# A hybrid attention, mLSTM and GLA layer: later decay broadcasts in the first block, a second buffer for convolution inputs, bias shifts spread over the gate projections

## The chip, the cores and the metric

The kernel runs on one core of a Trainium2 chip. The metric is device time in microseconds (us) of one execution, as the median of several runs. A core has TensorE (PE; its weight loads are shown apart as PEld), VectorE (DVE), ScalarE (ACT), GpSimd (POOL) and SyncE (SP), which here only issues DMAs. L123 is a line of the kernel before.

## What is computed

One layer on a sequence of 2048 rows of width 1024. All three head groups read the same normalised input, and their gated outputs go together through one output projection. Cut to its core:

```python
hn = rmsnorm(x, norm_g)
z = einsum('bsd,de->bse', hn, w_in)
(aq, ak, av, ag, mq, mk, mv, mo, mi, mf, mg, gq, gk, gv, ga, gg) = split(z)

# A: softmax attention over the own chunk of 64 and the 8 before, with a relative-position bias
y_a = band_chunk_attention(aq, ak, av, rel_bias) * silu(ag)

# B: mLSTM with exponential input gate, sigmoid forget gate and running-max stabiliser
qk = silu(causal_conv(concat([mq, mk]), conv_w))          # 4 taps along the sequence
y_b = sigmoid(mo) * head_rmsnorm(mlstm_chunkwise(mq_c, mk_c, mv, mi + b_i, mf + b_f), ml_norm_g) * silu(mg)

# C: gated linear attention with a decay for each key channel
log_alpha = log_sigmoid(ga @ w_alpha + b_alpha) / 16
y_c = head_rmsnorm(gla_chunkwise(gq, gk, gv, log_alpha), gla_norm_g) * silu(gg)

x = x + concat([y_a, y_b, y_c]) @ w_out
return rmsnorm(x, final_g)
```

## The kernel before

**Stages.** The first stage goes through the sequence in four blocks `q` of 512 rows. For each it makes the projections and runs the mLSTM and GLA recurrences in chunks of 128 rows; attention's queries, keys and values go to DRAM. The second stage does attention and the output projection block by block.

**Matmuls.** A projection is computed from high and low parts: the raw weights (128x1024 f32) are loaded by SyncE (L225), ScalarE casts them to the high part (L227), VectorE or GpSimd subtracts to get the low part (L228). Three matmuls for each of eight slices of the inner dimension then accumulate in a PSUM bank named `ip` (L236 to L238 in `proj_g`, L256 to L258 in `proj_t`). There are two `ip` banks, three buffers for raw weights and five for split ones. A bank is free again when its result has been read: by a copy (L513 and L515 for values, L547 for convolution inputs), a tanh (L486 in `sig_tile`) or a tanh and VectorE's product (L492 in `silu_tile`).

**Order.** PE's order is that in which the program is written. `Flow` weaves the recurrences, which are Python generators, into the projections: `flow.piece` counts PE's time and steps each chain that is due. On every other engine, SyncE among them, a list scheduler orders the instructions by priority and by its own estimate of when each is ready; what stands in `tc.high_priority` (casts, evacuations, raw loads) comes ahead, `tc.keep_in_program_order` pins an instruction, and `tc.issue_after(ins)` puts what is traced inside behind `ins` on `ins`'s engine. The hardware then runs each engine's list in that order.

**A block** runs, in program order: `proj_z` (GLA's query and key), `proj_v` (values for mLSTM, L256 to L258), `proj_gg` (GLA's gate), the second half of `proj_v`, `proj_m` (the mLSTM's queries and keys with their convolution), `prep_x` (loads of the next block's `x`, squares on ScalarE at L280, a diagonal `dg` at L285), then `proj_gm` (output gates `mo` and `mg`, three each), `prep` (the next block's input) and `proj_a` (attention's projections). `gates` of a block runs at its beginning; it writes the decay rows to `nm_d` in DRAM (L458) and turns gate rows by four transposes (L476). In the last block the order differs a little.

**What the change touches:**

- `load_dd` (L645 to L648), inside `mlstm`: broadcasts one chunk's six decay rows from `nm_d` to all 128 partitions (`dd`, 384 KB). L663 works on each of the six, L665 takes the exponential, L682 multiplies the scores. `mlstm` loads chunk 0 and 1 when it is first stepped, which is in `proj_gm` behind the load of `mo0`'s weights; in the scheduler's hands these DMAs may go out as soon as `nm_d` is written.
- `proj_m` (L540 to L561): for each of six tiles a copy of the bank to `zb`, 3 + 512 columns (L547), its three leading columns by GpSimd (L549 or L551), the last three kept for the next block (L552), the first tap on ScalarE (L554), three taps on VectorE (L556), tanh (L558) and product (L559). `zb` is the tile `u` with one buffer.
- `g_tile` (L203): tiles of 512 columns from `gpool`, which has five buffers, for `gates`, `prep`, `prep_x` and `prep_first`.
- `bias_rel` (L609 to L616), called in block `q == 1` ahead of `proj_gm`: loads attention's bias tile `bt` and shifts its six heads on ScalarE (L615), then GpSimd fills the masked corner (L616). Attention reads `bt` in the second stage.
- `gsel` (L434, L441): selects the gate rows; 64 columns for the mLSTM's.
- `Kt` (L194): seven key tiles for GLA, of which the first four use 64 of 128 columns (L831, L839).

Of the kernel before, what the change touches and what calls it, by code (L numbers as in the profile page):

```python
# [8 lines left out]
FP32 = mybir.dt.float32  # L9
FR = mybir.dt.float32r  # L10
AF = mybir.ActivationFunctionType
# [5 lines left out]
P = 128  # L17
D = 1024
KT = D // P
QT = 512  # L20
ST = 256
L = 128
# [79 lines left out]
def trunk_kernel(ctx: ExitStack, tc: tile.TileContext, xT, x, w_f, w_t, w_o, w_gates, norm_g, conv_w,  # L102
                 gate_sel, one_row, bias, ml_g, gla_g, final_g, out):
    nc = tc.nc
# [8 lines left out]
    nm_d = dram.tile([NQ, MH, QT], FP32, name="nm_d")  # L113
# [29 lines left out]
    with ExitStack() as pa_:  # L143
# [20 lines left out]
        onerow = one.tile([P, 1], FP32, name="onerow")  # L164
        gsel = one.tile([P, P + 64], FP32, name="gsel")
        zero6 = one.tile([P, 1], FP32, name="zero6")[G0:G0 + MH]
# [26 lines left out]
        glg = one.tile([P, 2], FP32, name="glg")  # L193
        Kt = one.tile([P, 7, P], FP32, name="Kt")  # L194
        nc.gpsimd.memset(Kt, 0.0)
        Qb = one.tile([P, 8, 4, 16], FP32, name="Qb")
# [6 lines left out]
        def g_tile(shape):  # L203
            return gpool.tile(shape, FP32, name="g")

# [13 lines left out]
        def load_w(src, k):  # L219
            if early_w:  # L220
                return early_w.pop(0)
            w = w_tile(k)
            with tc.high_priority(offset=AHEAD):
                raw = wraws.tile([P, D], FP32, name="wraw")
                nc.sync.dma_start(raw, src)  # L225
                rv = raw.rearrange("p (k n) -> p k n", k=k)
                nc.scalar.copy(w[:, :, 0, :], rv)  # L227
                other().tensor_tensor(w[:, :, 1, :], rv, f32(w[:, :, 0, :]), op=ALU.subtract)  # L228
            return w
# [13 lines left out]
        def proj_f(name, X):  # L243
            out_ = []
            for _ in proj_g(name, X, out_, 4):
                flow.piece(12 * 0.227)
            return out_[0]
# [183 lines left out]
        def gates(q, g1, R):  # L431
            t0 = q * QT
            pb = bank("pw")
            nc.tensor.matmul(pb[0:64], gsel[:, P:P + 64], g1, start=True, stop=True)  # L434
            gi = g_tile([P, QT])[G0:G0 + MH]
# [47 lines left out]
        def sig_tile(ps):  # L483
            th = ev.tile([P, QT], FP32, name="e")
            with tc.high_priority(offset=AHEAD):
                nc.scalar.activation(th, ps, AF.Tanh, scale=0.5)  # L486
            return th
# [52 lines left out]
        def proj_m(X):  # L540
            qk = big.tile([P, 6, QT], FP32, name="qk", bufs=1)
            tail = big.tile([P, 6, 3], FP32, name="tail")
            for b in range(6):
                ps = proj_f(("mq" if b < 3 else "mk") + str(b % 3), X)
                zb = big.tile([P, 3 + QT], FP32, name="u", bufs=1)
                with tc.high_priority(offset=AHEAD):
# [15 lines left out]

        def proj_gm(X):
            gm = big.tile([P, 3, QT], FP32, name="gm", bufs=1)
            for a in range(3):
                th = sig_tile(proj_f(f"mo{a}", X))
                nc.gpsimd.tensor_scalar(th, th, 1.0, mlg[:, a:a + 1], op0=ALU.add, op1=ALU.mult)
                sl = silu_tile(proj_f(f"mg{a}", X))
                nc.gpsimd.tensor_tensor(gm[:, a, :], th, sl, op=ALU.mult)
            return gm  # L570

# [37 lines left out]
        def bias_rel():  # L609
            bc = big.tile([P, AH], FP32, name="sm")  # L610
            nc.sync.dma_start(bc, bias[:, :, 256])
            nc.scalar.activation(bc, bc, AF.Copy, scale=-1.0)
            nc.sync.dma_start(bt, bias[:, :, 0:256])
            for h in range(AH):
                nc.scalar.activation(bt[:, h, :], bt[:, h, :], AF.Identity, bias=bc[:, h:h + 1])  # L615
            nc.gpsimd.memset(bt[0:64, :, 192:256], NEG)  # L616

        def m_tile(shape):
# [22 lines left out]
        def mlstm(q, qk, vs, R, held=None):  # L641
# [3 lines left out]
            def load_dd(c):  # L645
                dd = d_tile()
                nc.sync.dma_start(dd, nm_d[q, :, c * L:(c + 1) * L].partition_broadcast(P))
                return dd  # L648
# [162 lines left out]
        def gla(q, vg, gg, G, held=None):  # L811
            for sub in range(2):
# [7 lines left out]
                for c in range(2):  # L820
# [9 lines left out]
                    for i in range(1, 8):  # L830
                        nc.gpsimd.tensor_tensor(Kt[:, i - 1, 0:16 * i].rearrange("p (b j) -> p b j", j=16), ko[:, c, 0:i, :],  # L831
                                                Dt[:, c, i, 1:1 + i].unsqueeze(2).broadcast_to([P, i, 16]), op=ALU.mult)
# [4 lines left out]
                    for i in range(1, 8):  # L837
                        w = 64 if i < 5 else P
                        nc.tensor.matmul(of_ps[0:w, 64 * i:64 * i + 64], Kt[:, i - 1, 0:w], Qb[:, i, :, :].rearrange("p h i -> p (h i)"),  # L839
                                         start=True, stop=True)  # L840
# [63 lines left out]
        for q in range(NQ):  # L904
# [34 lines left out]
            flow.need("gates")  # L939
            if q == 1:  # L940
                bias_rel()
            M = dict(R)
            flow.start("mlstm", mlstm(q, qk, vs, M))
            M["gm"] = proj_gm(X)
            R = {}
# [325 lines left out]
def _layout(inputs):  # L1271
# [34 lines left out]
    o["conv_w"] = np.ascontiguousarray(a["conv_w"][0].reshape(4, 6, P).transpose(2, 1, 0))  # L1306
    gs = np.zeros((4, 32, P + 64), np.float32)
    gs[:, 0:16, 0:P] = a["w_alpha"][0]
# [5 lines left out]
    gs[0, 28, P + 32:P + 32 + MH] = a["b_gates"][0][:MH][[0, 2, 4, 1, 3, 5]]  # L1314
    gs = gs.reshape(P, P + 64)
    o["one_row"] = np.zeros((P, 1), np.float32)
# [29 lines left out]
```

## Time and profile before

| what | value |
|---|---|
| median of the three runs | 1284.47 us |
| these runs | 1284.54, 1284.47, 1280.35 us |
| the profiled execution's own time | 1278.8 us |
| its span | 1276.9 us |
| PE's granted clock in it | 0.99 |

The span is the part of the execution in which the program's instructions run. Busy time of PE counts the modelled ends of pipelined matmuls. In a timeline row stand start, length, engine, line, operation, tiles written and read, shape and count, and in brackets how long the engine had been idle and which instruction ended the wait. Rows of one engine in a row with the same work are merged, and their length then spans them all. In the chain of waits, one follows back from the last instruction what released each step.

### The profile page before, as it was taken

How to read it: one execution, taken by the hardware profiler on the slowest of the kernel's cores; microseconds unless marked ns; L12 is line 12 of the kernel's file. 1: busy time of each engine (PE TensorE's matmuls, PEld its weight loads, DVE VectorE, ACT ScalarE, POOL GpSimd, SP SyncE). 2: the span in 40 equal slices, each digit the busy share in tenths (PEclk: the TensorE clock that was granted, in tenths of full speed). 3: DMA queues.
4: the chain of work that ended last, by engine and by line, in shares of the span. 5: the costliest groups of instructions: out<-in, count | busy, mean ns of one | idle time of the engine just before them, and what ended most of it. 6: DMA issues, size and time to landing. Idle time of an engine off the chain costs nothing.

```text
span 1276.9 us, 19361 instructions
## 1 busy us (share of the span) xinstructions
PE 1243.8 (97%) x6804; PEld 1008.3 (79%) x6804; DVE 813.7 (64%) x1869; ACT 590.1 (46%) x1097; POOL 592.2 (46%) x761
## 2 busy tenths in 40 slices
PE   9999999999999999999999999999989999999997
PEld 7777777778777788877778877887867888878886
DVE  6647736772675878266577766675577677666641
ACT  5635432562533346254333643332576565655631
POOL 3336663233666232276622446642364454454442
PEclk7999999999999999999999999999999999999999
DMA  7157344324733442472344233526886456555122
GB/s 246 27 158 259 111 124 150 118 73 131 258 96 114 143 129 66 136 260 88 108 138 124 84 127 98 138 72 175 282 258 205 156 181 207 165 184 172 50 83 82
DMA packets 100185, 184.31 MB, mean 144 GB/s; under 512 B 10592, under 2 KB 46304, under 8 KB 100088
## 3 DMA queue, kind: packets, MB, share of 16 engines
q1 hardware_dynamic: 95624, 174.95, 43.6%
q10 hardware_dynamic: 4464, 8.13, 1.7%
q8 instruction: 53, 0.87, 0.3%
q14 instruction: 44, 0.36, 0.1%
HBM read 147.35 MB, written 35.70 MB: 143 GB/s over the span
## 4 chain that ended last, share of the span: by engine, by line
PE 77%; DVE 8%; POOL 4%; DMA 4%; issue 3%; ACT 3%; SPq 0%; POOLq 0%; DVEq 0%; ACTq 0%
PE ip L236 11%; PE ip L238 10%; PE ip L237 10%; PE ip L256 4%; PE ip L1196 4%; PE ip L1198 4%; PE ip L1197 4%; PE ip L258 4%; PE ip L257 4%; PE s L1055 4%; PE tp L1115 3%; DVE qk L556 2%; PE w L1134 2%; PE ga L839 2%; PE w L1131 2%
## 5 line engine op out<-in xcount | busy, mean ns | idle before, releaser
L236 PE MATMUL ip<-x,w 128*128 128x512 f32 x784 | 318.8, 407 | 3.0 <-ACT u L547 2.7
L238 PE MATMUL ip<-x,w 128*128 128x512 f32 x784 | 306.4, 391 | 0.0
L237 PE MATMUL ip<-x,w 128*128 128x512 f32 x784 | 306.0, 390 | 0.0
L236 PEld LDWEIGHTS ip<-x,w 128*128 128x128 f32 x784 | 147.3, 188 | 46.8 <-issue 12.5
L238 PEld LDWEIGHTS ip<-x,w 128*128 128x128 f32 x784 | 147.2, 188 | 32.4
L237 PEld LDWEIGHTS ip<-x,w 128*128 128x128 f32 x784 | 147.5, 188 | 28.1 <-issue 1.4
L227 ACT CAST w<-wraw 128x1024 fp32r<-128x1024 f32 x126 | 131.7, 1046 | 31.4 <-PE ip L258 10.3
L228 POOL TENSOR_TENSOR w<-wraw,w 128x1024 fp32r<-128x1024 f32 x42 | 100.8, 2401 | 97.0 <-ACT w L227 97.0
L228 DVE TENSOR_TENSOR w<-wraw,w 128x1024 fp32r<-128x1024 f32 x84 | 114.6, 1366 | 45.5 <-ACT w L227 45.4
L1076 POOL TENSOR_SCALAR pt<-pt,sm 128x640 f32<-128x640 f32 (+2 forms) x96 | 72.2, 754 | 118.9 <-DVE sm L1075 92.5
L256 PE MATMUL ip<-w,x 128*128 128x512 f32 x256 | 102.2, 399 | 4.4 <-DVE e L492 2.9
L258 PE MATMUL ip<-w,x 128*128 128x512 f32 x256 | 99.8, 390 | 0.0
L257 PE MATMUL ip<-w,x 128*128 128x512 f32 x256 | 99.7, 390 | 0.0
L781 POOL TENSOR_TENSOR prd<-gk,zg 128x16 f32<-128x16 f32 (+7 forms) x112 | 67.1, 599 | 68.0 <-PE pw L787 62.0
L1074 ACT ACTIVATE pt<-pt,sm 128x640 f32<-128x640 f32 (+2 forms) x96 | 73.3, 763 | 48.3 <-DVE sm L1071 43.9
L1122 DVE TENSOR_TENSOR pl<-tp,ph 128x512 fp32r<-128x512 f32 (+1 forms) x108 | 71.9, 672 | 35.0 <-ACT ph L1121 34.8
L1055 PE MATMUL s<-kk,qq 128*128 128x256 f32 (+2 forms) x360 | 82.4, 314 | 2.3 <-DVE sm L1071 2.2
L778 POOL TENSOR_TENSOR gk<-gk,al 128x16 f32<-128x16 f32 (+14 forms) x120 | 69.6, 580 | 22.1 <-ACT al L755 14.6
L1121 ACT CAST ph<-tp 128x512 fp32r<-128x512 f32 (+1 forms) x108 | 60.3, 572 | 39.7 <-PE tp L1115 37.3
L486 ACT ACTIVATE e<-ip 128x512 f32<-128x512 f32 x44 | 26.2, 595 | 107.5 <-PE ip L238 91.5
L1055 PEld LDWEIGHTS s<-kk,qq 128*128 128x128 f32 x360 | 62.8, 190 | 16.1 <-DVE sm L1071 5.8
L556 DVE SCALAR_TENSOR_TENSOR qk<-u,cw,qk 128x512 f32<-128x512 f32 x72 | 65.7, 913 | 13.7 <-ACT qk L554 12.2
(342 smaller groups left out, 2483.4 us busy)
## 6 DMA issues: line engine op xcount, KB each, us to landing
wraw<-in_w_f SPq DMA_DIRECT2D x100, 512.0 KB, 3.6
wraw<-in_w_t SPq DMA_DIRECT2D x28, 512.0 KB, 3.6
qq<-q_d SPq DMA_DIRECT2D x48, 256.0 KB, 4.8
kk<-k_d SPq DMA_DIRECT2D x18, 512.0 KB, 6.5
vv<-v_d SPq DMA_DIRECT2D x18, 512.0 KB, 5.8
xraw<-in_xT SPq DMA_DIRECT2D x16, 512.0 KB, 8.5
xr<-in_x SPq DMA_DIRECT2D x16, 512.0 KB, 3.7
out<-xr ACTq DMA_DIRECT2D x31, 256.0 KB, 2.2
```

The source lines that it names most:

```text
L227: nc.scalar.copy(w[:, :, 0, :], rv)
L228: other().tensor_tensor(w[:, :, 1, :], rv, f32(w[:, :, 0, :]), op=ALU.subtract)
L236: nc.tensor.matmul(ps, w[:, k, 0, :], X[k][:, 0, :], start=(k == 0), stop=False)
L237: nc.tensor.matmul(ps, w[:, k, 0, :], X[k][:, 1, :], start=False, stop=False)
L238: nc.tensor.matmul(ps, w[:, k, 1, :], X[k][:, 0, :], start=False, stop=(k == KT - 1))
L256: nc.tensor.matmul(ps, X[k][:, 0, t], w[:, 0, :], start=(k == 0), stop=False)
L257: nc.tensor.matmul(ps, X[k][:, 0, t], w[:, 1, :], start=False, stop=False)
L258: nc.tensor.matmul(ps, X[k][:, 1, t], w[:, 0, :], start=False, stop=(k == KT - 1))
L556: nc.vector.scalar_tensor_tensor(acc, zb[:, i:i + QT], cw[:, b, i:i + 1], acc, op0=ALU.mult, op1=ALU.add)
L1055: nc.tensor.matmul(sp[:, :cn], qq[:, l, tt * P:(tt + 1) * P], kk[:, ko + c0:ko + c0 + cn], start=(l == 0), stop=(l == 1))
L1074: nc.scalar.activation(pt[:, :n], pt[:, :n], AF.Exp, bias=init, scale=-1.0, accum_out=sm[:, 2:3])
L1076: nc.gpsimd.tensor_scalar(pt[:, :n], pt[:, :n], sm[:, 3:4], 0.5, op0=ALU.mult, op1=ALU.mult)
```

## The change

Three edits alter an order or a buffer. In the first block the broadcasts of chunks 0 and 1 are issued behind the last raw weights that were asked for; of the six convolution inputs the odd ones come from `gpool` instead of `u`; and `bias_rel` becomes a generator that is stepped once ahead of the mLSTM and then twice for each of the three pairs of gate projections, so that each shift stands behind a tanh. The other edits make tiles smaller or wider: `g` tiles have 515 columns, `gsel` loses 16, and `Kt` becomes four tiles of 64 columns and three of 128.

```diff
-        gsel = one.tile([P, P + 64], FP32, name="gsel")
+        gsel = one.tile([P, P + 48], FP32, name="gsel")
...
-        Kt = one.tile([P, 7, P], FP32, name="Kt")
-        nc.gpsimd.memset(Kt, 0.0)
+        Kh = one.tile([P, 4, 64], FP32, name="Kh")
+        nc.gpsimd.memset(Kh, 0.0)
+        Kl = one.tile([P, 3, P], FP32, name="Kt")
+        nc.gpsimd.memset(Kl, 0.0)
+        Kt = [Kh[:, i] for i in range(4)] + [Kl[:, i] for i in range(3)]
...
         def g_tile(shape):
-            return gpool.tile(shape, FP32, name="g")
+            t = gpool.tile([P, 3 + QT], FP32, name="g")[:, 0:QT]
+            return t.rearrange("p (c t) -> p c t", c=shape[1]) if len(shape) > 2 else t
...
                 raw = wraws.tile([P, D], FP32, name="wraw")
-                nc.sync.dma_start(raw, src)
+                st["raw"] = nc.sync.dma_start(raw, src).ins
...
-            nc.tensor.matmul(pb[0:64], gsel[:, P:P + 64], g1, start=True, stop=True)
+            nc.tensor.matmul(pb[0:48], gsel[:, P:P + 48], g1, start=True, stop=True)
...
-                nc.scalar.activation(th, ps, AF.Tanh, scale=0.5)
+                st["th"] = nc.scalar.activation(th, ps, AF.Tanh, scale=0.5).ins
...
-                zb = big.tile([P, 3 + QT], FP32, name="u", bufs=1)
+                zb = gpool.tile([P, 3 + QT], FP32, name="g") if b % 2 else big.tile([P, 3 + QT], FP32, name="u", bufs=1)
...
-        def proj_gm(X):
+        def proj_gm(X, shift=None):
             gm = big.tile([P, 3, QT], FP32, name="gm", bufs=1)
             for a in range(3):
                 th = sig_tile(proj_f(f"mo{a}", X))
+                if shift:
+                    next(shift)
                 nc.gpsimd.tensor_scalar(th, th, 1.0, mlg[:, a:a + 1], op0=ALU.add, op1=ALU.mult)
                 sl = silu_tile(proj_f(f"mg{a}", X))
                 nc.gpsimd.tensor_tensor(gm[:, a, :], th, sl, op=ALU.mult)
+                if shift:
+                    next(shift)
             return gm
...
             for h in range(AH):
-                nc.scalar.activation(bt[:, h, :], bt[:, h, :], AF.Identity, bias=bc[:, h:h + 1])
+                yield
+                with tc.issue_after(st["th"]):
+                    nc.scalar.activation(bt[:, h, :], bt[:, h, :], AF.Identity, bias=bc[:, h:h + 1])
             nc.gpsimd.memset(bt[0:64, :, 192:256], NEG)
+            yield
...
                 dd = d_tile()
-                nc.sync.dma_start(dd, nm_d[q, :, c * L:(c + 1) * L].partition_broadcast(P))
+                with tc.issue_after(st["raw"]) if q == 0 and c < 2 else nullcontext():
+                    nc.sync.dma_start(dd, nm_d[q, :, c * L:(c + 1) * L].partition_broadcast(P))
...
-                        nc.tensor.matmul(of_ps[0:w, 64 * i:64 * i + 64], Kt[:, i - 1, 0:w], Qb[:, i, :, :].rearrange("p h i -> p (h i)"),
+                        nc.tensor.matmul(of_ps[0:w, 64 * i:64 * i + 64], Kt[i - 1], Qb[:, i, :, :].rearrange("p h i -> p (h i)"),
...
-            if q == 1:
-                bias_rel()
+            shift = bias_rel() if q == 1 else None
+            if shift:
+                next(shift)
             M = dict(R)
             flow.start("mlstm", mlstm(q, qk, vs, M))
-            M["gm"] = proj_gm(X)
+            M["gm"] = proj_gm(X, shift)
```

More of the change, by code (lines that the diff above doesn't have):

```diff
@@ L830, in gla @@
                     for i in range(1, 8):
-                        nc.gpsimd.tensor_tensor(Kt[:, i - 1, 0:16 * i].rearrange("p (b j) -> p b j", j=16), ko[:, c, 0:i, :],
+                        nc.gpsimd.tensor_tensor(Kt[i - 1][:, 0:16 * i].rearrange("p (b j) -> p b j", j=16), ko[:, c, 0:i, :],
                                                 Dt[:, c, i, 1:1 + i].unsqueeze(2).broadcast_to([P, i, 16]), op=ALU.mult)
@@ L1306, in _layout @@
     o["conv_w"] = np.ascontiguousarray(a["conv_w"][0].reshape(4, 6, P).transpose(2, 1, 0))
-    gs = np.zeros((4, 32, P + 64), np.float32)
+    gs = np.zeros((4, 32, P + 48), np.float32)
     gs[:, 0:16, 0:P] = a["w_alpha"][0]
@@ L1314, in _layout @@
     gs[0, 28, P + 32:P + 32 + MH] = a["b_gates"][0][:MH][[0, 2, 4, 1, 3, 5]]
-    gs = gs.reshape(P, P + 64)
+    gs = gs.reshape(P, P + 48)
     o["one_row"] = np.zeros((P, 1), np.float32)
```

## The prediction

> **What bounds the kernel now.** I read the page first, then the list of what TensorE waited for, then the timelines of the engines around each of its waits.
>
> ```profile
> span 1276.9 us, 19361 instructions
> PE 1243.8 (97%) x6804; PEld 1008.3 (79%) x6804; DVE 813.7 (64%) x1869; ACT 590.1 (46%) x1097; POOL 592.2 (46%) x761
> ```
>
> TensorE (PE) is busy for 97% of the span, its instruction order is written by hand, and the change removes none of its matmuls. So the time can only fall by the length of waits on PE, at most the 33.1 us between 1276.9 and 1243.8. Which waits these are is told by the waits of PE alone (who waited for whom, us in total, times, longest):
>
> ```profile
> PE ip L256 <- DVE e L492: 2.9, 1, 2.9
> PE ip L236 <- ACT u L547: 2.7, 2, 2.5
> ...
> PE ip L256 <- ACT vg L515: 1.4, 1, 1.4
> ```
>
> Beside them the list has mostly waits of the attention stage, which no line of the diff touches. These three rows are waits for one of the two `ip` banks in which projections accumulate: the engine that should empty the bank came late. Together they hold 7.0 us in four waits, and each has a cause that the diff names.
>
> Wait 1, in the first block. SyncE's timeline, ScalarE's, the chain of waits (start, length, what) and PE's timeline:
>
> ```profile
> 59.89 0.97 SPq L647 DMA_DIRECT2D dd<-nm_d  x2
> 61.60 0.35 SPq L225 DMA_DIRECT2D wraw<-in_w_t  x1
> ```
> ```profile
> 60.44 1.14 DVE w L228
> ...
> 61.60 8.03 DMA wraw<-in_w_t
> ```
> ```profile
> 69.65 1.04 ACT L227 CAST w<-wraw 128x1024 fp32r<-128x1024 f32 x1 [6.19 <-DMA wraw<-in_w_t]
> 70.60 0.59 ACT L486 ACTIVATE e<-ip 128x512 f32<-128x512 f32 x1
> ```
> ```profile
> 68.88 0.39 PE L238 MATMUL ip<-x,w 128*128 128x512 f32 x1
> 69.11 0.60 PE L476 MATMUL pw<-ident,rows 128*128 128x128 f32 x4
> 72.61 0.50 PE L256 MATMUL ip<-w,x 128*128 128x512 f32 x1 [2.90 <-DVE e L492]
> ```
>
> Two decay broadcasts are issued at 59.89, and the raw weights right behind them take 8.03 us to land. ScalarE stands 6.19 us at the cast of those weights; the tanh that empties the bank of `gg0` (L486) is queued behind that cast, VectorE's L492 behind the tanh, and PE behind L492.
>
> Wait 2, in the second block: six bias shifts in a row on ScalarE, ahead of the copy that frees a bank.
>
> ```profile
> 271.11 2.50 ACT L615 ACTIVATE bt<-bt,sm 128x256 f32<-128x256 f32 x6
> ...
> 273.89 0.24 ACT L515 COPY vg<-ip 128x128 f32<-128x128 f32 x1
> ```
> ```profile
> 274.19 0.50 PE L256 MATMUL ip<-w,x 128*128 128x512 f32 x1 [1.40 <-ACT vg L515]
> ```
>
> Waits 3 and 4, in the third block's convolutions: `u` has one buffer, so the copy of the next convolution input waits until VectorE has read the last one.
>
> ```profile
> 559.08 1.06 ACT L280 ACTIVATE xraw<-xraw 128x1024 f32<-128x1024 f32 x1 [1.56 <-DMA xraw<-in_x]
> 560.05 0.19 ACT L280 ACTIVATION_READ_ACCUMULATOR xraw<-xraw 128x1 f32 x1
> 560.14 0.57 ACT L547 COPY u<-ip 128x512 f32<-128x512 f32 x1
> ...
> 569.19 0.58 ACT L547 COPY u<-ip 128x512 f32<-128x512 f32 x1 [5.36 <-DVE qk L556]
> ```
> ```profile
> 569.83 0.50 PE L236 MATMUL ip<-x,w 128*128 128x512 f32 x1 [2.53 <-ACT u L547]
> 576.32 0.50 PE L236 MATMUL ip<-x,w 128*128 128x512 f32 x1 [0.19 <-ACT u L547]
> ```
>
> **The change part by part.** The recorded waits are 2.90, 1.40, 2.53 and 0.19, together 7.02 us. A recorded wait begins at a matmul's modelled end, 0.39 us after its start, while the next one follows 0.23 after it (68.88 and 69.11 above). For the two waits behind a 512-column matmul of the same stream (2 and 3) I therefore add 0.16 each, and for wait 1 the same for its transposes: 7.5 us are there to be had.
>
> *Broadcasts behind the raw weights.* Nothing is removed; two DMAs and what hangs on the first (six L663, one exponential) move later. Without them the weights still can't be issued before 61.60, since their buffer comes free only with the L228 of 60.44. But they then have the DMA engines nearly alone:
>
> ```profile
> wraw<-in_w_t SPq DMA_DIRECT2D x28, 512.0 KB, 3.6
> ```
> ```profile
> dd<-nm_d SPq DMA_DIRECT2D x16, 384.0 KB, 5.8
> ```
>
> Landing after 3.6 instead of 8.03 us is 4.4 us sooner: the cast starts at 65.2, and the bank is free at 72.61 - 4.4 = 68.2, before PE wants it at 69.5 (69.11 and four transposes of 0.11). The whole wait goes, 2.90 + 0.16 = 3.06 us; the next bank, that of `gg1`, is wanted one tile of 5.5 us later. The margin is 1.3 us: a landing after 66.5 costs one for one, and I keep a loss of 1 us as the lower end.
>
> The broadcasts come out behind the weights of `mo0`, whose three loads are issued from 93.81 to 98.37, so among the loads of the next block's `x`. Queued behind them on SyncE are the next raw weights (`mg0`), which PE wants only after all six convolution tiles. Their work on VectorE then falls in the convolutions:
>
> ```profile
> 98.42 2.28 SPq L279 DMA_DIRECT2D xraw<-in_x  x4
> ```
> ```profile
> 100.00:145.00 45.00, 44.81 (x237) 34.82 (x235) 32.87 (x45) 24.68 (x43) 30.93 (x48) 1.00 0.56 197
> ```
> ```profile
> L663 DVE SCALAR_TENSOR_TENSOR dd<-dd,rt,cap 128x128 f32<-128x128 f32 x96 | 29.7, 377 | 0.5 <-DMA dd<-nm_d 0.4
> ```
> ```profile
> 141.56 2.56 DVE L559 SCALAR_TENSOR_TENSOR qk<-e,qk 128x512 f32<-128x512 f32 x1 [0.70 <-ACT e L558]
> ```
> ```profile
> 145.04 0.94 PE L670 MATMUL s<-qk 64*128 64x128 f32 x12
> ```
>
> Six at 377 ns are 2.3 us on VectorE, which has 45.0 - 32.9 = 12.1 us idle in that window (the window's row gives its length, then busy time and count of PE, weight loads, VectorE, ScalarE, GpSimd). Hidden there they cost nothing. If all of them land in front of the last convolution, which ends at 144.12 with 0.9 us to spare before the scores, they cost 2.3 - 0.9 = 1.4 us. Below nothing I exclude, as no work is removed. I take 0.5, nearer to the idle share.
>
> *Bias shifts.* The six of 2.50 us leave 271.11, so L515 comes up to 2.5 us earlier and the wait of 1.40 + 0.16 = 1.56 us goes. Afterwards each one stands behind a tanh of a gate projection. ScalarE there:
>
> ```profile
> 366.00:402.00 36.00, 11.04 (x20) 1.00 0.30 89
> ```
>
> 11.0 of 36 us are busy, so six pieces of 0.42 us (2.50 by six) lie beside matmuls, and each follows the operation that PE waits for. Cost 0; with no idle time behind the tanh it would be 0.42 us each, 2.5 us in all. The two bias loads and the mask go unnoticed: attention reads `bt` only in the last stage.
>
> *Two convolution inputs.* Odd tiles take theirs from `gpool`, whose five buffers the gates have long finished with at that time. Copies no longer wait for the previous convolution, only for the one before it.
>
> ```profile
> L556 DVE SCALAR_TENSOR_TENSOR qk<-u,cw,qk 128x512 f32<-128x512 f32 x72 | 65.7, 913 | 13.7 <-ACT qk L554 12.2
> ```
>
> Three L556 at 0.913 us are 2.7 us of VectorE, against 24 x 0.23 = 5.5 us of matmuls per tile, so VectorE keeps up on average and the one buffer was what stalled. Waits 3 and 4 go: 2.69 + 0.19 = 2.9 us. What is next is ScalarE itself, standing at L280 for `x` (1.56 us in the row above); if that holds the copies back as much as the buffer did, this gain is nothing.
>
> *The rest* (48 instead of 64 gate columns, `Kt` in two tiles, wider `g` tiles) changes widths of weight loads and start-up fills, while PE streams the same columns: 0.
>
> Sum: 3.06 + 1.56 + 2.88 - 0.5 = 7.0 us. The profiled execution took 1278.8 us (1276.9 of span and 1.9 around it), which gives 1271.8. The runs shown have a median of 1284.47, 5.7 above it, which gives 1277.5; the mean of all four executions, 1282.0, gives 1275.0. I take 1276.5.
>
> **Rivals.** *B, the broadcasts now land late.* Issued behind four loads of `x`, they share the DMA engines with 2 MB:
>
> ```profile
> DMA to landing us min/median/max: 5.9/7.7/11.3
> ```
> ```profile
> DMA to landing us min/median/max: 4.6/5.8/8.0
> ```
> ```profile
> 108.80 0.57 ACT L547 COPY u<-ip 128x512 f32<-128x512 f32 x1
> ```
> ```profile
> 112.78 0.50 PE L236 MATMUL ip<-x,w 128*128 128x512 f32 x1
> ```
>
> (The first is L279's, the second L647's.) From 100.8 by 7.7 and then 8.0 more, the first lands at 116.5. If L663 stands in VectorE's order among the convolutions, VectorE waits there, the tanh on ScalarE waits for VectorE, and the copy of 108.80 behind that tanh; PE wants its bank at 112.78. With 1.2 us for tanh and copy, PE loses 116.5 + 1.2 - 112.8 = 4.9 us: 1281.4. For it: in wait 1 ScalarE stood in just this way behind a cast whose data had not landed. Against it: VectorE need not meet L663 before the `x` loads have passed. The Trainium skill, "DMA: Bandwidth & Descriptors", section "Rules for kernel authors", speaks for B: it says to issue a DMA early and to wait for it late, and the change does the reverse. The trace has one broadcast issued early, and there the early issue is what delayed PE.
>
> *C, the second input isn't used in the place that counts*, because ScalarE's order keeps the copy of 560.14 behind the L280 of 559.08. Then waits 3 and 4 stay: 1276.5 + 2.9 = 1279.4.
>
> *D, slower.* B's mechanism at its upper end: the broadcasts issued after the four `xT` loads as well. VectorE's hold costs PE nothing until 111.6 (112.8 - 1.2) and one for one from there; beyond 111.6 + 7.0 = 118.6 the whole gain is gone. Landing at 100.8 + 11.3 + 11.3 + 4.6 = 128, it costs 16 us, of which convolutions that may now run ahead return perhaps one tile's 5.5: 1276.5 + 11 = 1287.5.
>
> *E, the change doesn't do what it says*: only PE's order is written down, the other engines' orders are re-planned, and a shift or a broadcast can come out ahead of another bank's copy. Then one wait is exchanged for another of the same 7.0 us: 1283.5.
>
> **How the numbers follow.** Chances: forecast 0.55, B 0.15, C 0.13, D 0.07, E 0.10. The forecast's own range is 1272 to 1281 (the two bases, 1275.0 and 1277.5, with 3 us each side for the costs above); B and C lie in it or at its end, E within 1286. So 1271 to 1286. About 0.5%, 6.4 us, is what a measurement of this kernel can tell from no change, so faster means below 1278.0: the forecast lies 1.5 us under that, and I give it 0.8 of its chance there, 0.44, with 0.05 from B and C: 0.49. Slower means over 1290.9: the upper part of D and E, 0.06. The rest, 0.45, is within 0.5%.
>
> **What would show it.** Right: in the changed kernel's list of PE's waits the rows for L492 and L515, and for the copy of the convolution input, are gone or under 0.3 us; the raw weights after 61 us land in about 4 us; six single shifts stand between 360 and 400 us. Wrong: VectorE's L663 shows a wait for its DMA near 105 us (B, D), L547 still waits for L556 and PE for it near 565 us (C), or a new row of over 1 us stands among PE's waits (E).

## The result, and the profile after

| | before | after |
|---|---|---|
| median of six runs each | 1282.43 us | 1273.57 us |
| lowest and highest | 1279.36 and 1285.72 us | 1272.03 and 1274.40 us |
| ratio after/before, 95% interval | | 0.9932 [0.9919, 0.9946] |
| profiled execution, its span | 1278.8, 1276.9 us | 1273.61, 1271.7 us |

The change makes the kernel 8.9 us faster (6.9 to 10.4 by the interval). In this section and the next, line numbers are those of the kernel that the fence belongs to; in the changed kernel nearly all have moved down by 4 to 13 (L492 is L496 there, L515 is L519, L547 is L551).

The page of the changed kernel, busy time. PE's busy time is where it was (1243.8 before); the span of the profiled execution is 5.2 us shorter, so the time came out of PE's waits:

```profile
PE 1243.1 (98%) x6804; PEld 1009.3 (79%) x6804; DVE 813.6 (64%) x1869; ACT 590.2 (46%) x1097; POOL 594.4 (47%) x762
```

The waits of PE in the changed kernel (who for whom, us in total, times, longest):

```profile
PE w L1144 <- ACT ph L1134: 5.0, 3, 3.8
...
PE pw L799 <- POOL prd L793: 1.8, 1, 1.8
```

All three rows that the prediction started from are gone from the head of the list: none for the product of `silu_tile`, none for the convolution input, and of those for `vg` there is one of 0.2 us. A new row has come in, L799 waiting for GpSimd. It is GLA's matmul on the products `prd` that GpSimd makes.

Wait 1. SyncE's, ScalarE's and PE's timelines of the changed kernel:

```profile
60.35 0.36 SPq L229 DMA_DIRECT2D wraw<-in_w_t  x1
...
97.65 5.03 SPq L659 DMA_DIRECT2D dd<-nm_d  x2
```
```profile
64.00 1.05 ACT L231 CAST w<-wraw 128x1024 fp32r<-128x1024 f32 x1 [1.79 <-DMA wraw<-in_w_t]
```
```profile
67.61 0.39 PE L242 MATMUL ip<-x,w 128*128 128x512 f32 x1
67.84 0.60 PE L480 MATMUL pw<-ident,rows 128*128 128x128 f32 x4
68.19 0.48 PE L260 MATMUL ip<-w,x 128*128 128x512 f32 x1
```

The raw weights issued at 60.35 land within 3.65 us instead of 8.03, ScalarE stands 1.79 us at their cast instead of 6.19, and L260 follows the transposes with no wait in brackets. The broadcasts go out at 97.65.

Wait 2, in two rows of ScalarE (the first and the last of six shifts, at 358.00, 363.94, 371.38, 381.90, 387.40 and 395.22) and one of PE, the matmul that waited 1.40 us before:

```profile
358.00 0.50 ACT L625 ACTIVATE bt<-bt,sm 128x256 f32<-128x256 f32 x1
...
395.22 0.51 ACT L625 ACTIVATE bt<-bt,sm 128x256 f32<-128x256 f32 x1
```
```profile
268.08 0.39 PE L260 MATMUL ip<-w,x 128*128 128x512 f32 x1
```

Wait 3, PE in the third block, and then the new wait:

```profile
559.28 0.39 PE L240 MATMUL ip<-x,w 128*128 128x512 f32 x1
...
564.81 0.61 PE L799 MATMUL pw<-prd,hs 128*32 128x208 f32 x6
567.21 0.62 PE L799 MATMUL pw<-prd,hs 128*32 128x256 f32 x2 [1.79 <-POOL prd L793]
```

**Where the time came from.** Since PE's order is fixed, the same matmul can be looked up in both traces, and the difference of its two starts is the running gain. These two rows of before show waits in the second block that the prediction had not listed; the fence behind them has the same matmuls in the changed kernel:

```profile
354.73 0.33 PE L834 MATMUL gb<-ident,dr 128*128 128x128 f32 x1 [0.20 <-ACT dr L791]
...
365.44 0.67 PE L857 MATMUL ga<-Sbd,q 128*128 128x256 f32 x2 [0.61 <-DVE at L851]
```
```profile
347.95 0.27 PE L846 MATMUL gb<-ident,dr 128*128 128x128 f32 x1
...
357.85 0.59 PE L869 MATMUL ga<-Sbd,q 128*128 128x256 f32 x2
```

| matmul, by its place before | start before, after | running gain | gained here |
|---|---|---|---|
| last one ahead of the transposes of wait 1 | 68.88, 67.61 | 1.27 | 1.27, start-up |
| behind wait 1 | 72.61, 68.19 | 4.42 | 3.15 |
| ahead of wait 2 | 272.40, 267.86 | 4.54 | 0.12 |
| behind wait 2 | 274.19, 268.08 | 6.11 | 1.57 |
| second block, L834 | 354.73, 347.95 | 6.78 | 0.67 |
| second block, L857 | 365.44, 357.85 | 7.59 | 0.81 |
| ahead of wait 3 | 566.91, 559.05 | 7.86 | 0.27 |
| behind wait 3 | 569.83, 559.28 | 10.55 | 2.69 |
| behind the new wait and a stretch at half the clock | 600.05, 593.05 | 7.00 | -3.55 |
| last block's projections, ahead of attention | 929.97, 922.27 | 7.70 | 0.70 |
| end of the span | 1276.9, 1271.7 | 5.2 | -2.5 |

The 1.27 us of the start-up are not the change's. They arise between 17 and 23 us, where PE's granted clock was 0.50 in the kernel before and 0.87 in the changed one. Two profiles of one and the same kernel, e_tail and e_tail2 below, differ there as much (the granted clock stands third from the end: 0.50 and 0.82), and the matmul that starts at 68.88 before starts at 68.90 in one and at 67.41 in the other:

```profile
17.00:23.00 6.00, 5.36 (x15) 4.21 (x15) 5.79 (x9) 4.73 (x8) 2.33 (x2) 0.50 1.07 373
```
```profile
17.00:23.00 6.00, 5.36 (x25) 4.33 (x24) 5.56 (x9) 4.27 (x7) 1.81 (x2) 0.82 1.07 380
```

So 10.55 us were gained by the third block, 9.28 of them behind the start-up. Of the 5.35 given back, 1.95 went into the new wait of L799 (1.79 by its row, and 0.16 since the row counts from a modelled end), some 1.6 into a stretch at half the clock right behind that (last section), and 2.5 into the attention stage, while the fourth block gained 0.70. From 930 us to the end each of the 13 other profiles of this study loses 1.5 to 4.5 us against that of before (e_mem, which has none of the three reorderings, 2.2), so that loss tells of before's profiled execution and not of the change. The largest wait of the attention stage is 5.0 us here and, in the row of before below, 3.8:

```profile
PE w L1131 <- ACT ph L1121: 3.8, 3, 2.3
```

That wait had between 3.7 and 6.6 us in the profiles of all the kernels of this study, in no order with their edits; the diff touches nothing of it. The profiled execution of before, 1278.8 us, lies below the lowest of its six runs in the comparison, while that of the changed kernel lies on its median. So the spans differ by 5.2 us where the medians differ by 8.9; the medians are the measure.

### The profile page after: what moved, and what is told of

Its sections match the earlier page's. It is cut to its first block, busy times and chain, and to the rows that moved or that the text cites. A ratio compares the mean times of both kernels' runs of the same rounds, so it can differ in the third digit from the quotient of the medians.

```text
span 1271.7 us, 19323 instructions
## 1 busy us (share of the span) xinstructions
PE 1243.1 (98%) x6804; PEld 1009.3 (79%) x6804; DVE 813.6 (64%) x1869; ACT 590.2 (46%) x1097; POOL 594.4 (47%) x762
## 4 chain that ended last, share of the span: by engine, by line
PE 89%; DVE 3%; POOL 3%; DMA 2%; issue 1%; ACT 1%; SPq 1%; POOLq 0%; DVEq 0%; ACTq 0%
PE ip L240 14%; PE ip L241 13%; PE ip L242 13%; PE ip L260 4%; PE ip L261 4%; PE ip L262 4%; PE ip L1209 4%; PE ip L1211 4%; PE ip L1210 4%; PE s L1068 4%; PE tp L1128 3%; PE ga L851 2%; PE w L1147 2%; PE s L705 2%; PE w L1144 2%
## 5 line engine op out<-in xcount | busy, mean ns | idle before, releaser
L260 PE MATMUL ip<-w,x 128*128 128x512 f32 x256 | 102.0, 398 | 0.0
L1128 PE MATMUL tp<-ident,pt 128*128 128x128 f32 x420 | 62.5, 274 | 2.5 <-POOL pt L1089 2.5
```

The source lines that it names most:

```text
L260: nc.tensor.matmul(ps, X[k][:, 0, t], w[:, 0, :], start=(k == 0), stop=False)
L1128: nc.tensor.transpose(out=tp[:, w + x_ * P:w + (x_ + 1) * P], in_=pt[:, (b - b0) * P:(b - b0 + 1) * P], identity=ident)
```

## The experiments

Each ran beside the kernel before on the same chip, the first four over three rounds and the others over five; the ratio is to that kernel. In the text a gain is (1 - ratio) times its median there (1281.41, 1281.12 and 1282.02 us for the three groups).

The theory to be tested was that of the prediction: three causes, each with its own wait, whose prices add up. The rivals were that the broadcasts come late and hold VectorE (B), and that an edit only exchanges one wait for another (E).

| kernel | ratio [95%] | gain, us |
|---|---|---|
| e_bcast: broadcasts alone | 1.0005 [0.9991, 1.0019] | -0.6 |
| e_conv: second convolution input alone, with the tile sizes | 0.9981 [0.9964, 0.9998] | 2.4 |
| e_bias: spread shifts alone | 0.9986 [0.9974, 0.9999] | 1.8 |
| e_mem: tile sizes alone | 0.9993 [0.9980, 1.0007] | 0.9 |
| e_again: the whole change again | 0.9936 [0.9917, 0.9956] | 8.2 |
| e_bc: the change without the spread shifts | 0.9945 [0.9927, 0.9962] | 7.0 |
| e_early: broadcasts behind the last weights of `proj_v` | 0.9975 [0.9960, 0.9990] | 3.2 |
| e_tail: the change, small copies on ScalarE | 0.9924 [0.9907, 0.9941] | 9.7 |
| e_hold: broadcasts alone, chunk 0's six held back | 0.9957 [0.9940, 0.9974] | 5.5 |
| e_one: only chunk 1's broadcast later | 0.9973 [0.9960, 0.9987] | 3.5 |
| e_best: e_tail with e_early's place | 0.9921 [0.9901, 0.9941] | 10.1 |
| e_tail2: e_tail again | 0.9924 [0.9907, 0.9941] | 9.7 |

### e_bcast, the broadcasts alone

```diff
-                nc.sync.dma_start(raw, src)
+                st["raw"] = nc.sync.dma_start(raw, src).ins
...
-                nc.sync.dma_start(dd, nm_d[q, :, c * L:(c + 1) * L].partition_broadcast(P))
+                with tc.issue_after(st["raw"]) if q == 0 and c < 2 else nullcontext():
+                    nc.sync.dma_start(dd, nm_d[q, :, c * L:(c + 1) * L].partition_broadcast(P))
```

> The kernel before with the later broadcasts alone. If the gains are three separate waits of PE that add up: the 2.9 us wait for VectorE's L492 near 72 us is gone, the waits for the bias shifts' neighbour (1.4 us) and for the convolution input (2.5 us) stay, and the time falls by about 3 us. If the gain of the whole change comes from a re-planned order of the other engines instead, the wait may go but the time moves by less than 1 us or by an amount that no wait of the list explains.

Measured: 1281.68 us, ratio 1.0005 [0.9991, 1.0019]; the gain of wait 1 doesn't reach the end. Wait 1 itself is gone: ScalarE's cast starts at 63.50 instead of 69.65. What has come in its place, in the timelines of VectorE, ScalarE and PE:

```profile
63.50 1.05 ACT L227 CAST w<-wraw 128x1024 fp32r<-128x1024 f32 x1 [1.81 <-DMA wraw<-in_w_t]
...
116.29 0.58 ACT L547 COPY u<-ip 128x512 f32<-128x512 f32 x1 [2.92 <-DVE qk L556]
```
```profile
108.16 0.75 DVE L556 SCALAR_TENSOR_TENSOR qk<-u,cw,qk 128x512 f32<-128x512 f32 x1 [0.36 <-ACT qk L554]
108.83 3.66 DVE L664 SCALAR_TENSOR_TENSOR dd<-dd,rt,cap 128x128 f32<-128x128 f32 x6
...
113.25 0.74 DVE L556 SCALAR_TENSOR_TENSOR qk<-u,cw,qk 128x512 f32<-128x512 f32 x1
...
115.44 0.74 DVE L556 SCALAR_TENSOR_TENSOR qk<-u,cw,qk 128x512 f32<-128x512 f32 x1
```
```profile
116.92 0.50 PE L236 MATMUL ip<-x,w 128*128 128x512 f32 x1 [3.37 <-ACT u L547]
```

Read it from the bottom. PE waits 3.37 us for a bank that the copy into `u` should have emptied; the copy starts 0.11 us behind the third tap of the convolution before it, which ends at 116.18, since `u` has one buffer. Between the first tap (108.16) and the second (113.25) stand the six operations on the broadcast that has just landed (L664 here, L663 before), for 3.66 us. They wait for no DMA: the row of 108.83 has no bracket. So it isn't rival B's late landing that costs here; the six are in the middle of a convolution that has no second buffer. Behind the wait PE runs for a while at half the clock (last section). By PE's running gain e_bcast has its 3.15 us behind wait 1, like the changed kernel, and loses 4.9 between 113 and 150 us: 3.5 of it in this wait, the rest at the half clock.

### e_conv and e_mem, the second input and the tile sizes

e_mem has the smaller `gsel`, the divided `Kt` and the `g` tiles of 515 columns and nothing else. e_conv has these, which make room, and

```diff
-                zb = big.tile([P, 3 + QT], FP32, name="u", bufs=1)
+                zb = gpool.tile([P, 3 + QT], FP32, name="g") if b % 2 else big.tile([P, 3 + QT], FP32, name="u", bufs=1)
```

> The kernel before with the smaller gate and key tiles and the wider g tiles alone, so with none of the three reorderings. If widths and places in memory cost nothing: the same three waits on PE with the same lengths and a time within 1 us of the kernel before. If the places in memory matter (start-up, GpSimd beside VectorE), the time moves by over 2 us and the waits by over 0.5 us.

Measured: 1280.62 us, ratio 0.9993 [0.9980, 1.0007]. The sizes alone can't be told from nothing, and the three waits stay, at 2.8, 1.8 and 1.4 us. The middle one, for the convolution input, is 0.7 us shorter than before, which was not expected. In the kernels of this study with one buffer it lies between 1.7 and 2.5 us, with that of before at the upper end.

> The kernel before with the second convolution input alone, and the smaller gate and key tiles that make room for it. If the waits add up: the 2.5 us wait for the copy of the convolution input in the third block is gone, the other two stay, and in the third block PE then waits about 1.8 us for GpSimd's GLA products (prd) as in the changed kernel, with some 1.3 us of half clock behind it; the time falls by 0 to 2 us. If the new wait for GpSimd belongs to another of the edits, it is not there and the time falls by about 3 us.

Measured: 1278.27 us, ratio 0.9981 [0.9964, 0.9998]. Waits of PE in e_conv:

```profile
PE ip L260 <- DVE e L496: 2.8, 1, 2.8
...
PE pw L791 <- POOL prd L785: 1.5, 1, 1.5
PE ip L260 <- ACT vg L519: 1.4, 1, 1.4
```

Waits 1 and 2 stay, that for the convolution input is gone, and the new wait for GpSimd's `prd` is here already, this time without the half clock behind it. It belongs to the second input and not to the broadcasts or the shifts: PE comes sooner to the same place in the third block, and GpSimd isn't ready.

### e_bias, the spread shifts alone

The generator `bias_rel`, `st["th"]` and the two `next(shift)` in `proj_gm`, as in the diff of the change; nothing else.

> The kernel before with the spread bias shifts alone. If the waits add up: the 1.4 us wait for the values' copy near 274 us is gone, the other two stay, and the time falls by about 1.6 us; the six shifts stand singly between 360 and 405 us and none of them is waited for. If shifts among the gate projections hold back the banks there, PE shows new waits of 0.4 us each near 370 to 405 us and the time falls by less than 0.5 us.

Measured: 1279.49 us, ratio 0.9986 [0.9974, 0.9999], a gain of 1.8 us (0.1 to 3.3) where the wait was worth 1.56. Waits of PE in e_bias, in which the row for `vg` no longer shows:

```profile
PE ip L256 <- DVE e L492: 2.8, 1, 2.8
...
PE ip L236 <- ACT u L547: 2.1, 2, 1.9
```

### e_again and e_bc, do the parts add up?

e_again is the changed kernel once more. e_bc is the changed kernel with the six shifts in one piece again:

```diff
             for h in range(AH):
-                yield
-                with tc.issue_after(st["th"]):
-                    nc.scalar.activation(bt[:, h, :], bt[:, h, :], AF.Identity, bias=bc[:, h:h + 1])
+                nc.scalar.activation(bt[:, h, :], bt[:, h, :], AF.Identity, bias=bc[:, h:h + 1])
...
-            shift = bias_rel() if q == 1 else None
-            if shift:
-                next(shift)
+            if q == 1:
+                bias_rel()
+            shift = None
```

> The changed kernel once more, beside the others. If the wait of 1.8 us for GpSimd's GLA products in the third block belongs to the order of its instructions, it is there again with 1.5 to 2.2 us; the half clock behind it (3.4 us long) may come or not. The ratio to the kernel before is 0.992 to 0.995.

Measured: 1272.97 us, ratio 0.9936 [0.9917, 0.9956], as at first; the new wait for `prd` comes again, with 1.5 us.

> The changed kernel with the bias shifts back in one piece, so later broadcasts and second convolution input together. Theory: the late broadcasts stop VectorE in the first block's convolutions, which costs PE 3.4 us with one input buffer and nothing with two; then no wait near 117 us, the 1.4 us wait near 270 us is back, and the time is about 1.6 us above the changed kernel and 6 us or more below the kernel before, which is more than the two edits gave alone (0 and 2.4 us). Rival: the parts simply add up with scatter, then the ratio to the kernel before is 0.997 to 0.999, near the product of the two alone.

Measured: 1274.17 us, ratio 0.9945 [0.9927, 0.9962], a gain of 7.0 us (4.9 to 9.4). Broadcasts and second input together bring 7.0 us, where alone they brought -0.6 and 2.4. Waits of PE in e_bc:

```profile
PE ip L260 <- ACT vg L519: 1.4, 1, 1.4
PE pw L796 <- POOL prd L790: 1.4, 1, 1.4
```

There is no wait of 3.4 us for a convolution input in the first block. The changed kernel shows why, in its own rows of VectorE and ScalarE for that place:

```profile
108.10 0.75 DVE L560 SCALAR_TENSOR_TENSOR qk<-g,cw,qk 128x512 f32<-128x512 f32 x1 [0.36 <-ACT qk L558]
109.03 3.51 DVE L675 SCALAR_TENSOR_TENSOR dd<-dd,rt,cap 128x128 f32<-128x128 f32 x6 [0.19 <-DMA dd<-nm_d]
```
```profile
108.48 0.59 ACT L551 COPY u<-ip 128x512 f32<-128x512 f32 x1 [0.42 <-PE ip L242]
```

The six stand at the same place and take as long. But the convolution they interrupt reads from a `g` tile, so the copy into `u` goes out at 108.48 and PE's bank is free. The same 3.5 us of VectorE cost PE 3.4 us with one buffer and nothing with two.

### e_hold and e_one, two other ways round the same clash

If the six inside the convolution are the whole of what e_bcast lost, then with one buffer still, moving them behind the convolutions must bring the gain out. e_hold is e_bcast with

```diff
-                nc.vector.scalar_tensor_tensor(acc, th, 1.0, acc, op0=ALU.add, op1=ALU.mult)
+                st["conv"] = nc.vector.scalar_tensor_tensor(acc, th, 1.0, acc, op0=ALU.add, op1=ALU.mult).ins
...
-            behind = None
+            behind = st["conv"] if q == 0 else None
```

so that chunk 0's six (L664 here) are issued behind the last L559 of the block.

> The later broadcasts alone (one input buffer), with the first chunk's six L663 on VectorE held behind the first block's last convolution. Theory: the wait of 3.4 us near 117 us came from these six (3.7 us of VectorE in the middle of the second convolution, their data already there); so it falls below 1 us, the scores of chunk 0 lose at most 1.5 us near 145 us, and the time is 1.5 to 4 us below the kernel before. Rival: the wait came from the transfers themselves (the broadcasts among the loads of x, which delay ScalarE's squares and so the copy); then over 2 us of it stay and the time is that of the kernel before.

Measured: 1277.40 us, ratio 0.9957 [0.9940, 0.9974], a gain of 5.5 us (3.3 to 7.7). VectorE in e_hold:

```profile
140.28 2.56 DVE L559 SCALAR_TENSOR_TENSOR qk<-e,qk 128x512 f32<-128x512 f32 x1 [0.69 <-ACT e L558]
142.76 2.09 DVE L664 SCALAR_TENSOR_TENSOR dd<-dd,rt,cap 128x128 f32<-128x128 f32 x6
```

The six now run at 142.76, no wait is left near 117 us, and PE doesn't wait for them at the scores either. So the same late broadcasts, with the same one buffer, bring nothing with the six inside a convolution and something with them behind it. The gain is larger than was expected, and why it is larger than wait 1 stays open; its interval reaches down to 3.3, close to the 3.06 of that wait, and in its profile PE is 3.0 us ahead of before at 600 us, start-up apart.

e_one leaves chunk 0's broadcast where it was and sends only chunk 1's later (`q == 0 and c == 1` in e_bcast's condition).

> The kernel before with only chunk 1's broadcast issued later; chunk 0's stays ahead of the weights. Theory: wait 1 is the time that the broadcasts' bytes take from the weights behind them; with half of them the weights land 2 to 3 us sooner (5 to 6 us instead of 8) and PE's wait of 2.9 us falls below 1 us, while no wait of over 1.5 us stands near 117 us; the time falls by 2 to 3 us. Rival: what counts is that SyncE waits for the decay rows before it issues anything; then the wait stays at over 2 us.

Measured: 1278.06 us, ratio 0.9973 [0.9960, 0.9987], a gain of 3.5 us. The weights are issued at 60.05, and ScalarE's row gives their landing:

```profile
65.75 1.05 ACT L227 CAST w<-wraw 128x1024 fp32r<-128x1024 f32 x1 [3.83 <-DMA wraw<-in_w_t]
```

So they take 8.03 us behind two broadcasts, 5.7 behind one, and 3.65 behind none (in the changed kernel). Behind one, PE still waits 0.55 us of the 2.90 (its L256 of 68.70), and chunk 0's six stand at 71 us, ahead of the convolutions:

```profile
71.28 3.31 DVE L664 SCALAR_TENSOR_TENSOR dd<-dd,rt,cap 128x128 f32<-128x128 f32 x6
```

### e_early, another place for the broadcasts

e_bcast with the broadcasts issued behind the last weights of the second half of `proj_v`, not those of `mo0`:

```diff
             ws = [load_w(w_t[j, g], 2) for g in range(4)]
+            st["wt"] = st.get("raw")
...
-                with tc.issue_after(st["raw"]) if q == 0 and c < 2 else nullcontext():
+                with tc.issue_after(st["wt"]) if q == 0 and c < 2 else nullcontext():
```

> The kernel before with the first block's broadcasts issued behind the last raw weights of the second half of proj_v, so some 5 us later than before and not 35. Theory: wait 1 came from broadcasts ahead of weights in SyncE's queue, and the new wait near 117 us of the later broadcasts from their landing among the convolutions; so both are gone here, wait 1 is under 0.5 us, and the time falls by about 3 us with one input buffer. Rival: the DMA engines' share is what counts, not the order; then the weights still land after more than 6 us and over 1.5 us of wait 1 stay.

Measured: 1278.24 us, ratio 0.9975 [0.9960, 0.9990], a gain of 3.2 us. SyncE in e_early:

```profile
59.31 0.35 SPq L225 DMA_DIRECT2D wraw<-in_w_t  x1
...
62.24 0.96 SPq L649 DMA_DIRECT2D dd<-nm_d  x2
```

The weights that PE waits for go out first at 59.31 and the broadcasts 2.9 us behind, so wait 1 goes, and chunk 0's six, at 70.57, come before the convolutions and clash with nothing. The gain (1.3 to 5.1 by the interval) agrees with wait 1's own price, 3.06 us. A wait of 1.4 us for GLA's `dr` stands at 126 us in this kernel, as in several others.

### e_tail, e_tail2 and e_best, the new wait

In the changed kernel GpSimd, ahead of the `prd` that PE waits for at 567.21:

```profile
561.98 0.18 POOL L555 COPY u<-tail 128x3 f32<-128x3 f32 x1
...
562.67 0.65 POOL L555 COPY g<-tail 128x3 f32<-128x3 f32 x1
563.28 0.62 POOL L793 TENSOR_TENSOR prd<-gk,zg 128x240 f32<-128x240 f32 x1
563.84 1.18 POOL L556 COPY tail<-g 128x3 f32<-128x3 f32 x1
564.98 1.13 POOL L790 TENSOR_TENSOR gk<-gk,al 128x240 f32<-128x240 f32 x1
566.19 0.97 POOL L793 TENSOR_TENSOR prd<-gk,zg 128x256 f32<-128x256 f32 x1
```

GpSimd goes from one operation to the next without a pause, and among GLA's operations stand copies of 128x3 elements that take 0.18, 0.65 and 1.18 us. e_tail moves both kinds to ScalarE:

```diff
-                    nc.gpsimd.tensor_copy(zb[:, 0:3], st["zb"][:, b, :])
-                nc.gpsimd.tensor_copy(tail[:, b, :], zb[:, QT:QT + 3])
+                    nc.scalar.copy(zb[:, 0:3], st["zb"][:, b, :])
+                nc.scalar.copy(tail[:, b, :], zb[:, QT:QT + 3])
```

> The changed kernel with the two small copies at each convolution input (its three leading columns and the three kept for the next block) on ScalarE and not on GpSimd. Theory: in the third block GpSimd is what ends last, and these copies stand in its queue ahead of the GLA products; then PE's wait of 1.8 us there falls below 0.7 us and the time by 1 to 3 us against the changed kernel. Rival: the products wait for VectorE's share of the port and not for the queue; then over 1.3 us of the wait stay and the time is within 1 us.

Measured: 1271.60 us, ratio 0.9924 [0.9907, 0.9941], beside 1272.97 for e_again on the same chip. GpSimd and PE in e_tail:

```profile
565.25 1.66 POOL L793 TENSOR_TENSOR prd<-gk,zg 128x256 f32<-128x256 f32 x1
```
```profile
566.96 0.62 PE L799 MATMUL pw<-prd,hs 128*32 128x256 f32 x2 [0.26 <-POOL prd L793]
```

> The changed kernel with the small copies on ScalarE once more, beside the one with both edits. Ratio to the kernel before 0.991 to 0.994, no wait for GpSimd's products of over 0.7 us in the third block.

Measured: 1272.06 us, ratio 0.9924 [0.9907, 0.9941]; the wait is 0.9 us this time, more than the 0.7 expected. In the profiles the wait went from 1.8 and 1.5 us (twice the changed kernel) to 0.3 and 0.9 (twice e_tail). The medians agree with that, by 1.4 us within one group, but the intervals overlap: a gain of this size isn't shown by the times. Nor did GpSimd get back all that the copies took: from the end of its last weight subtraction (561.02) to the end of the `prd` that PE waits for (567.16) it needs 6.1 us in the changed kernel and 5.5 in e_tail and e_tail2, as the last `prd` took 1.66 us there instead of 0.97.

e_best is e_tail with the broadcasts at e_early's place.

> The changed kernel with both extra edits: the small copies on ScalarE, and the first block's broadcasts behind the last weights of proj_v. Theory: the broadcasts' new place gains nothing over the other once there are two input buffers, so the time is within 1 us of the kernel with the small copies on ScalarE alone (1271 to 1272 us). Rival: the six L663 at VectorE's idle time near 73 us free the convolutions further, and the time is 1 to 2 us lower.

Measured: 1271.53 us, ratio 0.9921 [0.9901, 0.9941], the same as e_tail2 on the same chip. With two buffers the later place of the broadcasts costs nothing that the earlier one could give back.

## Why the prediction was right, and where it wasn't

**The forecast's mechanism holds.** The three waits and their disappearance are shown in the changed kernel's profile, and each one's cause by the experiment that had its edit alone. By the running gains, wait 1 gave 3.15 us (3.06 in the sum), wait 2 gave 1.57 (1.56) and wait 3 gave 2.69 (2.69); wait 4's 0.19 lies at the place of the new wait and can't be told apart. The cost of 0.5 us for the moved broadcasts doesn't show: the running gain is the same at 150 us as behind wait 1 (4.42). The sum of 7.0 us lies at the lower end of the ratio's interval. The time that was forecast, 1276.5, is 2.9 us above the median measured. It stands for a base of 1283.5 less 7.0; the base measured is 1282.43, which is 1.1 of the 2.9, and the gain measured is 8.9, which is the other 1.9.

**What made the gain larger than the sum.** Two waits of the second block, 0.20 and 0.61 us in before's rows, were not listed; their places gave 0.67 and 0.81 us. The second, at L857, is gone in e_conv, e_bc and every other kernel with the second input, and in none with one buffer: it goes with the second input, though how was not followed up. The first, at L834, is gone in e_mem, e_bias and e_early too, so it doesn't need the second input. The prediction took only the waits whose row named the copy of the convolution input.

**What is luck in the number.** Start-up and attention apart, the profiled pair gained 7.4 us in the three waits and 2.6 at places that the prediction hadn't listed, and lost 3.55 in the new wait and the half clock behind it, which it hadn't listed either: 6.4 us in all. That the sum of 7.0 lies near this owes something to two omissions that nearly cancel. Where the rest of the median's 8.9 comes from, one profile of each kernel doesn't show.

**The step that failed is the independence of the terms.** The sum priced the moved L663 at 0.5 us, with 12.1 us of idle time on VectorE as their cover and 1.4 as the upper end, "if all of them land in front of the last convolution". There the six took 3.5 to 3.7 us and not 2.3, and their worst place was another: inside a convolution, where a single `u` hands VectorE's delay to ScalarE's copy and so to PE. e_bcast measured this at the whole of the gain, and e_hold and e_one showed that it goes when the six stand elsewhere. The forecast came out right because the second input, added as a separate term, is also the cover of the first. Counted apart, the two edits bring 1.8 us; together 7.0.

**Rival B** had the right place and the wrong cause. VectorE did meet the six among the convolutions near 105 to 109 us, but waited 0.19 us for the DMA in the changed kernel and not at all in e_bcast. The margin is thin all the same: the two broadcasts are issued from 97.65, and VectorE's six start at 109.03, so the first took 11.4 us to land, where the prediction's row had a median of 5.8. The Trainium skill, "DMA: Bandwidth & Descriptors", section "Rules for kernel authors", with its advice to issue early and wait late, would have the earlier place be better; e_early, against e_bcast, agrees with it by 3.8 us (gains of 3.2 and -0.6), but e_best against e_tail2 shows no difference, and the broadcasts at their place before, earlier than both, are what delayed the weights.

**Rival C** is refuted by the trace: no wait is left at 559.28. The copy does stand right behind the squares, as C said (L551 at 554.26, behind the L284 of 553.22), but it ends at 554.83, 4.5 us before PE wants the bank. **Rival D** needed a landing near 118.6 us; the measured one is 109. **Rival E** happened on a small scale, and its sign, a new row of over 1 us, is there: the wait for `prd`. It wasn't a re-planned order but the next engine in line. GpSimd had GLA's chain and the small copies of the convolution to do, and PE coming sooner found it late. The prediction asked what is late next for VectorE and ScalarE only.

**The base.** The profiled execution of before was one of the quickest of its kernel; with the median the prediction made up for that, and the measured difference of the medians bears it out.

## What to carry to other kernels

Before adding up what several edits should save, ask of each what covers its cost, and whether another edit provides that cover: here moving the transfers to this place was worth nothing without a second buffer and 4.6 us with it (7.0 less the 2.4 of the buffer alone). Where work moves on an engine that is idle a quarter of the time, look at which operation it lands between, and who holds a single buffer meanwhile. And when a wait of the bounding engine goes, list the arrival times of all the other engines at the next place, down to their three-column copies, since the first of them that is late is the new wait.

## What the runs showed of the hardware that was not expected

**Half the clock behind short waits.** The granted clock of PE falls to 0.50 for about 3.4 us after some waits and not after others. The windows of the changed kernel behind its wait of 1.79 us, and of e_again behind the same wait of 1.45 us (window, length, then busy time and count of PE, weight loads, VectorE, ScalarE and GpSimd, granted clock, DMA share, GB/s):

```profile
568.00:569.00 1.00, 1.00 (x4) 0.76 (x4) 0.98 (x1) 1.00 (x3) 0.96 (x1) 0.55 0.07 29
569.00:571.00 2.00, 2.00 (x6) 1.60 (x5) 1.97 (x4) 0.40 (x1) 1.92 (x4) 0.50 0.41 96
571.00:572.00 1.00, 1.00 (x5) 0.73 (x4) 0.96 (x2) 0.00 (x0) 0.92 (x2) 0.75 0.74 299
```
```profile
568.00:570.00 2.00, 2.00 (x10) 1.67 (x9) 2.00 (x3) 1.06 (x3) 2.00 (x3) 1.00 0.07 16
```

At half clock the matmuls of 512 columns start 0.43 us apart (568.52, 568.95, 569.38 in the changed kernel) instead of 0.23; the counts in the rows take in those that reach into a window. Taken together the three windows have 0.9, 2.0 and 0.5 us of it, 3.4 in all or eight matmuls, which costs some 1.6 us. Behind e_bcast's wait of 3.37 us it shows as well:

```profile
117.00:121.50 4.50, 4.50 (x13) 3.54 (x14) 3.77 (x4) 2.25 (x4) 2.68 (x4) 0.62 0.28 98
```

(4.5 us at 0.62 is again 3.4 us at half.) Behind the wait of 2.53 us in the kernel before there is none:

```profile
570.00:572.00 2.00, 2.00 (x10) 1.62 (x10) 1.66 (x2) 1.85 (x3) 1.84 (x4) 1.00 0.03 12
```

So 1.79 us of waiting brought it on in one execution and 2.53 didn't in another; 1.84 us did in e_mem, at the matmul of 569.29, and 1.93 didn't in e_bias, at 569.17. Whether a wait under 3.4 us costs 1.6 us more is chance as far as these runs tell, and so is the start-up, where one kernel ran at 0.50 and at 0.82 and its profiles came to differ by 1.5 us. The Trainium skill, "TensorE: Matmul & The Clock Gate", section "What's actually happening", gives a window of 3413 ns that runs freely, and the 3.4 us measured agree with its length; its section "Why this matters for your kernels" asks for no idle gaps of over about 3 us, and with that the case of 1.79 us doesn't agree.

**Transfers behind others.** 512 KB of weights landed after 3.65 us, or after 5.7 or 8.03 with one or two broadcasts of 384 KB issued just ahead of them on the same engine's queue: 2.1 and 2.3 us for each broadcast.

**Small copies on GpSimd.** In the rows shown above, a copy of 128x3 took GpSimd 0.18 us at 561.98 and 1.18 at 563.84. ScalarE in e_tail does such a copy in 0.19:

```profile
565.14 0.19 ACT L556 COPY tail<-g 128x3 f32<-128x3 f32 x1
```

What slowed GpSimd's there wasn't tried.
